# A hybrid decoder step on one core: output projection by halves of the tokens, per-layer projection in two parts, and a last FFN group of four tiles

## The chip, the core and the metric

The kernel runs on one core of one Trainium2 chip. Its engines are TensorE (PE in the profile, with its weight loads as PEld), VectorE (DVE), ScalarE (ACT), GpSimd (POOL) and SyncE (SP); all DMAs of this kernel are started on SP's queue. The metric is the device time of one execution in microseconds (us); less is better.

## The reference

One layer of a decoder step for 1024 prompt tokens and 8 sample tokens, 1032 columns in all, with a model width of 1024. Two branches (a Mamba-2 SSD and a gated delta net, GDN) are projected, gated and merged. Then follow an output projection with a residual, a SwiGLU FFN of width 2816, an embedding per layer and a final norm. The end of the layer, where the change lies:

```python
mix = (g_ssm * jnp.einsum('ble,ed->bld', y.astype(dtype), w_branch_ssm)
       + g_gdn * jnp.einsum('ble,ed->bld', o.astype(dtype), w_branch_gdn))
x = x + jnp.einsum('bld,de->ble', mix, w_out)

gu = jnp.einsum('bld,df->blf', _rms_norm(x, norm_ffn), w_ffn_in)
gt, up = jnp.split(gu, 2, axis=-1)
x = x + jnp.einsum('blf,fd->bld', jax.nn.silu(gt) * up, w_ffn_out)

pe = jnp.einsum('blp,pd->bld', p, w_pl_proj)
x = x + pe * jax.nn.sigmoid(jnp.einsum('bld,de->ble', _rms_norm(x, norm_pl), w_pl_gate))
```

## The kernel before

**Layout.** Activations lie with the channels on the 128 partitions and the 1032 tokens (`NT`) along the free axis; 1024 channels are 8 tiles. Every product is made in three matmuls: each operand is split in a high part (rounded to `float32r`) and a low remainder, and high x high, high x low and low x high are summed in PSUM. `dense` does this for one block of 128 output columns, by chunks of tokens: `CHUNKS` are three of 344, `PARTS` are 384, 384 and 264. A block's sums go to PSUM tiles `pd` (three banks); the other PSUM pools are `pt` (2), `py` (2) and `pz` (1).

**Weights.** `load_w` loads a block of weights into a tile `wraw` (two buffers) and `split_raw` makes a high part `wh` on ACT and a low part `wl` on DVE, four 128x128 blocks at a time, with three buffers of each. This is done at a raised priority.

**Order of the work.** The tile framework makes the order of each engine's instructions ahead of the run, from the order of the code, the priorities and its own model of the costs; on the chip each engine and each queue then runs its list in order, and waits on semaphores.

**The stages around the change**, in the order of the code:

1. `ssm_branch(3, yacts)`: the last quarter of the SSM branch product. `load_o` loads the eight GDN outputs `o` and their gates, multiplies and splits them.
2. Branch merge: for each of 8 output blocks, the gates `sg_d` are loaded, the block's product with `w_branch_gdn` is made, and the merged block is split into `macts` (tiles `mx`). `residual` loads and transposes the input `x` into `acc`, called `x2` from here on.
3. Output projection: for each `f` of 8, `dense(load_w(w_out...), macts, ev)`, the sum added to `x2`. `squares` sums the squares of the channels for the norm: ACT squares, POOL adds into `sqs` (the last block's go to `rb`). Between the blocks, `embed` loads the per-layer embeddings by 128 tokens (`pr`), transposes and splits them into `pacts`.
4. `roots`: POOL adds `sqs` to `rb`, PE sums over the partitions with a matrix of ones, ACT takes the root and DVE the reciprocal.
5. The per-layer projection: for each of 8 blocks a product of `pacts` with `w_pl_proj`, copied by ACT to the tile `pe` and stored to `pe_d` in DRAM, to be read in the last stage.
6. FFN input. The product of the normed `x2` with `w_ffn_in` is made by a Strassen-like scheme on 2x2 blocks (halves of the channels and halves of the tokens, `HALF`, 516 tokens each): seven products instead of eight for each of the `NF` = 22 column tiles. Its seven operands are `b11`, `b21`, `bt1` to `bt4` and `b22`. `put` splits an operand (ACT, then DVE); the sums and differences are made on POOL. This preparation is a loop over `k` of 4, with single-buffered tiles `n1`, `n2`, `t1` to `t4`. `ffn_in(i)` makes the weights' combinations and the seven products, in chunks of 258; `product` takes the PSUM banks in turn from the list `spaces`. `b11` and `b21` need the first half of the tokens alone, and the first two products (`w11`, `w12`) need only these.
7. FFN output: after `ffn_in(i)` for even `i` from 2, `ffn_out(i - 2)` multiplies a pair of tiles `gu` (three buffers in the pool `gp`) with `w_ffn_out` and adds to `x2`. The last group (tiles 20 and 21) is a loop of its own with `PARTS`; there `gain_split` makes the operands `h3` of the next stage and the squares of the last-but-one norm.
8. The gate product with `w_pl_gate` (weights `gw`), the sum of `pe` times its sigmoid, and the final norm.

`bq` are two large tiles in the place of the two tiles `o`; `b11`, `b21`, `bt2` and `bt3` are their quarters. `pacts` lies in the quarter `bt3`, and is overwritten there once the per-layer projection is done with it.

## Time and profile before

| | us |
|---|---|
| median of 3 runs | 2696.67 |
| lowest and highest of them | 2696.55, 2699.24 |
| the profiled execution | 2692.9 |
| its span, first to last instruction | 2691.2 |
| output projection, start and end | 1715 to 1808 |
| last FFN group, first to last matmul | 2540.5 to 2577.8 |

Mean granted TensorE clock over the span: 0.987. DMA: 306.50 MB, mean 114 GB/s.

How to read the rows in this document. In a page's busy times the share is of the span. In a table by window, each row has the window, its length, the busy time of each engine with its number of instructions, the granted TensorE clock, the mean busy share of the 16 DMA engines and GB/s. In a list of waits, `A <- B: us, times, longest us` says that A's engine sat idle until B. In a timeline or a chain, a row has a start, a length, the engine, the line of the kernel, the operation, output<-inputs, the shape and a count, and in brackets the idle time ahead and what ended it. Groups of instructions give count, then busy time in us, the mean of one in ns, and the idle time ahead. Matmuls overlap, so a price is taken from start to start or over a long row.

### The profile page before, as it was taken

How to read it: one execution, taken by the hardware profiler on the slowest of the kernel's cores; microseconds unless marked ns; L12 is line 12 of the kernel's file. 1: busy time of each engine (PE TensorE's matmuls, PEld its weight loads, DVE VectorE, ACT ScalarE, POOL GpSimd, SP SyncE). 2: the span in 40 equal slices, each digit the busy share in tenths (PEclk: the TensorE clock that was granted, in tenths of full speed). 3: DMA queues.
4: the chain of work that ended last, by engine and by line, in shares of the span. 5: the costliest groups of instructions: out<-in, count | busy, mean ns of one | idle time of the engine just before them, and what ended most of it. 6: DMA issues, size and time to landing. Idle time of an engine off the chain costs nothing.

```text
span 2691.2 us, 46064 instructions
## 1 busy us (share of the span) xinstructions
PE 2591.2 (96%) x17959; PEld 2500.6 (93%) x17959; DVE 1761.8 (65%) x3217; ACT 1104.2 (41%) x2304; POOL 400.1 (15%) x599
## 2 busy tenths in 40 slices
PE   7999999999999999999999999996999999999988
PEld 7999999989989899898999999996999999999988
DVE  6677897588557576565445565337766666666775
ACT  5555555455364373343342234324322222322343
POOL 0111222121110110210000000025111111111020
PEclk9999999999999999999999999997999999999999
DMA  3345445445453453477664366222211111111132
GB/s 124 118 153 171 132 163 150 106 116 161 103 133 114 106 148 104 104 203 205 189 192 141 116 193 195 81 70 81 59 48 48 48 58 54 48 48 48 42 90 94
DMA packets 457384, 306.50 MB, mean 114 GB/s; under 512 B 44753, under 2 KB 430714, under 8 KB 456142
## 3 DMA queue, kind: packets, MB, share of 16 engines
q1 hardware_dynamic: 454766, 295.13, 38.0%
q10 hardware_dynamic: 2400, 8.42, 0.8%
q8 instruction: 142, 2.33, 0.4%
q14 instruction: 76, 0.62, 0.1%
HBM read 227.17 MB, written 76.31 MB: 113 GB/s over the span
## 4 chain that ended last, share of the span: by engine, by line
PE 62%; DMA 6%; DVE 6%; ACT 4%; issue 1%; POOL 1%; SPq 1%; DVEq 0%; POOLq 0%; ACTq 0%
PE pd L69 44%; PE py L69 7%; PE pt L69 6%; PE pz L69 3%; DMA ab<-acum_d 2%; ACT ab L709 1%; DVE wl L139 1%; DMA out_dram<-so 1%; ACT wh L138 1%; DVE bq L1220 1%; ACT sdt L613 0%; DMA sg<-gate_d 0%; DMA srb<-rn_d 0%; DVE sd L614 0%; DMA at<-at_d 0%
## 5 line engine op out<-in xcount | busy, mean ns | idle before, releaser
L69 PE MATMUL pd<-h,wh 128*128 128x344 f32 x4272 | 1041.1, 325 | 15.6 <-ACT wh L138 9.1
L69 PEld LDWEIGHTS pd<-h,wh 128*128 128x128 f32 x4272 | 740.6, 189 | 28.3 <-ACT wh L138 11.4
L69 PE MATMUL pd<-h,wl 128*128 128x344 f32 x2136 | 691.9, 324 | 3.3 <-DVE wl L139 2.3
L139 DVE TENSOR_TENSOR wl<-wraw,wh 128x512 fp32r<-128x512 f32 (+1 forms) x346 | 244.2, 708 | 263.5 <-ACT wh L138 261.3
L138 ACT CAST wh<-wraw 128x512 fp32r<-128x512 f32 (+1 forms) x346 | 209.5, 608 | 502.8 <-PE pd L69 361.5
L69 PEld LDWEIGHTS pd<-h,wl 128*128 128x128 f32 x2136 | 404.2, 189 | 8.6 <-DVE wl L139 6.8
L69 PE MATMUL pd<-gu,wh 128*128 128x344 f32 (+2 forms) x1056 | 251.2, 321 | 11.3 <-DVE acc L1344 11.1
L69 PEld LDWEIGHTS pd<-gu,wh 128*128 128x128 f32 x1056 | 183.0, 189 | 13.1 <-DVE acc L1344 9.5
L69 PE MATMUL pd<-y,wh 128*128 128x344 f32 x768 | 185.3, 323 | 0.0
L69 PE MATMUL pd<-gu,wl 128*128 128x344 f32 (+1 forms) x528 | 169.8, 322 | 0.0
L1318 DVE TENSOR_TENSOR acc<-acc,pd 128x344 f32<-128x344 f32 x240 | 121.9, 511 | 59.3 <-PE pd L69 54.7
L69 PE MATMUL pd<-bq,wh 128*128 128x258 f32 (+1 forms) x624 | 130.1, 302 | 20.3 <-ACT pe L1214 12.0
L709 ACT ACTIVATE ab<-ab,ncolA 128x128 f32<-128x128 f32 x256 | 81.8, 391 | 137.9 <-POOL ab L705 137.8
L69 PEld LDWEIGHTS pd<-y,wh 128*128 128x128 f32 x768 | 132.4, 188 | 1.1 <-issue 0.2
L69 PEld LDWEIGHTS pd<-bq,wh 128*128 128x128 f32 x624 | 103.3, 197 | 24.4 <-ACT pe L1214 13.3
L422 ACT COPY raw<-pd 128x344 f32<-128x344 f32 x144 | 62.6, 438 | 151.4 <-PE pd L69 138.9
L69 PE MATMUL pd<-y,wl 128*128 128x344 f32 x384 | 123.8, 323 | 0.0
L69 PEld LDWEIGHTS pd<-gu,wl 128*128 128x128 f32 x528 | 99.7, 189 | 0.0
L69 PE MATMUL pd<-o,wh 128*128 128x344 f32 x384 | 93.8, 326 | 3.9 <-DVE o L186 1.8
L436 DVE SCALAR_TENSOR_TENSOR ca<-raw,cwm,ca 128x1056 f32<-128x1056 f32 x72 | 95.9, 1333 | 2.0
L436 DVE SCALAR_TENSOR_TENSOR ca<-raw,cwg,ca 128x1056 f32<-128x1056 f32 x72 | 96.7, 1343 | 0.8
L69 PE MATMUL pd<-h,gw 128*128 128x384 f32 (+1 forms) x576 | 95.4, 324 | 0.0
(480 smaller groups left out, 5187.4 us busy)
## 6 DMA issues: line engine op xcount, KB each, us to landing
wraw<-in_w_in_dram SPq DMA_DIRECT2D x88, 512.0 KB
ab<-acum_d SPq DMA_DIRECT2D x32, 512.0 KB
out_dram<-sd SPq DMA_DIRECT2D x48, 256.0 KB
ru<-in_w_ffn_in_dram SPq DMA_DIRECT2D x22, 512.0 KB
wraw<-in_w_ffn_in_dram SPq DMA_DIRECT2D x22, 512.0 KB
wro<-in_w_ffn_out_dram SPq DMA_DIRECT2D x80, 128.0 KB
sg_d<-mg SPq DMA_DIRECT2D x16, 516.0 KB
bb<-rk_d SPq DMA_DIRECT2D x8, 1024.0 KB
```

The lines of the kernel that those rows point to most:

```text
L69: TE.matmul(o, l, r, start=start, stop=stop)
L138: S.copy(wh[:, :n], raw[:, k0 : k0 + n])
L139: V.tensor_tensor(wl[:, :n], raw[:, k0 : k0 + n], wh[:, :n].bitcast(F32), ALU.subtract)
L422: S.copy(raw[:, 3 + t0 : 3 + t0 + n], o[:, :n])
L436: V.scalar_tensor_tensor(ca, raw[:, j : j + CONVN], w[j], ca, ALU.mult, ALU.add)
L709: S.activation(ab[:, h], ab[:, h], AF.Exp, bias=ncolA[:, c, h0 + h : h0 + h + 1])
L1220: V.tensor_tensor(q[:, 1, k], src, q[:, 0, k].bitcast(F32), ALU.subtract)
L1318: V.tensor_tensor(a, a, o, ALU.add)
```

## The change

- `squares`/`roots`: the addition of `sqs` and `rb` on POOL goes; PE adds them by two matmuls into one PSUM bank.
- The embeddings are loaded, transposed and split ahead of `ssm_branch(3)`, into two tiles `ple`, and stored in DRAM (`ple_d`); at the start of the output projection they are loaded back into the quarter `bt3`.
- The per-layer projection of blocks 0 to 3 stands between `ssm_branch(3)` and the branch merge (output in pairs of a tile `pe`), that of blocks 4 to 7 behind the output projection, with PSUM banks of three pools in turn (`fills`).
- The output projection runs twice over the 8 blocks, first for tokens 0 to 515 and then for the rest, each in two chunks of 258. Behind the first half, its roots are taken, the eight normed tiles of that half are made and put into `b11` and `b21`, and stored in DRAM (`n_d`).
- The preparation works on the second half alone: it loads the stored halves `n1`, `n2`, makes `m1`, `m2`, and from them the five other operands, in tiles with two buffers. Per `k`: three operations on DVE, three on POOL, five `put`.
- The first two products of FFN tiles 0 and 1 (`ffn_first`) stand directly behind this preparation in the code, ahead of the rest of `ffn_in(0)`.
- The last group takes four tiles (18 to 21) with four weight blocks each; `ffn_out(18)` goes. The tile `gu` of number 21 lies in the place of `rb` and `sqs` (tile `rs`), the gate weights and the last-but-one norm's tiles move.

The diff, cut to what matters (plain moves of `product` and `plus` out of `ffn_in` are left out):

```diff
-            ps = pd.tile([P, 512], F32, name="pd")
+            pool, name = (pd, "pd") if pools is None else pools[0]
+            if pools is not None:
+                pools.append(pools.pop(0))
+            ps = pool.tile([P, 512], F32, name=name)
...
+    pacts = []
+    for k in range(2):
+        t = part_tile("ple")
+        pacts.append((t[:, 0], t[:, 1], t))
+    for tt in range(9):
+        n = P if tt < 8 else NB
+        pr_ = b2.tile([P, 256], F32, name="pr", tag="xf")
+        dma(pr_[:n], p_prompt[0, 0, tt * P : tt * P + P, :] if tt < 8 else p_sample[0, :, 0, :])
+        t = pt.tile([P, 512], F32, name="pt")
+        ts = slice(tt * P, tt * P + n)
+        for k in range(2):
+            TE.transpose(t[:, k * P : k * P + n], pr_[:n, k * P : k * P + P], ident[:n, :n])
+            hilo(pacts[k][0][:, ts], pacts[k][1][:, ts], t[:, k * P : k * P + n])
+    for k in range(2):
+        dma(ple_d[k], pacts[k][2].bitcast(F32))
     ssm_branch(3, yacts)
...
+    def per_layer(f, pacts, t, pools):
+        def ev(t0, tn, o):
+            S.copy(t[:, t0 : t0 + tn], o)
+
+        dense(load_w(w_pl_proj[:, f * P : f * P + P], 2), pacts, ev, CHUNKS, pools)
+        dma(pe_d[f], t)
+
+    for f in range(4):
+        if f % 2 == 0:
+            pe_ = part_tile("pe", F32)
+        per_layer(f, [a[:2] for a in pacts], pe_[:, f % 2], None)
...
-        G.tensor_tensor(rb[:, ts], rb[:, ts], sqs[:, ts], ALU.add)
-        mm(t[:, :tn], ones, rb[:, ts])
+        mm(t[:, :tn], ones, sqs[:, ts], True, False)
+        mm(t[:, :tn], ones, rb[:, ts], False, True)
...
+    rs = nrm.tile([P, 2, NT], F32, name="rs")
+    rb, sqs = rs[:, 0], rs[:, 1]
...
     QT = NT // 2
+    QC = QT // 2
...
+    b11, b21, bt2, bt3 = bq[0][:, 0], bq[0][:, 1], bq[1][:, 0], bq[1][:, 1]
+    pv = bt3.rearrange("p h (k two) t -> p h k (two t)", two=2)
     pacts = [(pv[:, 0, k], pv[:, 1, k]) for k in range(2)]
...
-        dense(load_w(w_out[:, f * P : f * P + P], 8), macts, ev)
-        if f < 7:
-            squares(f, sqs, rb, 0, NT, b2)
-        if 1 <= f < 6:
-            embed(2 * f - 2)
-            if f < 5:
-                embed(2 * f - 1)
+    for k in range(2):
+        dma(pv[:, :, k].bitcast(F32), ple_d[k])
+
+    def put(q, k, src):
+        S.copy(q[:, 0, k], src)
+        V.tensor_tensor(q[:, 1, k], src, q[:, 0, k].bitcast(F32), ALU.subtract)
+
+    def scaled(dst, j, ts):
+        V.scalar_tensor_tensor(dst, x2[:, j, ts], gain(G_FFN, j), rb[:, ts], ALU.mult, ALU.mult)
+
+    for hf in range(2):
+        parts = tuple((hf * QT + c * QC, QC) for c in range(2))
+        for f in range(8):
+            def ev(t0, tn, o):
+                a = x2[:, f, t0 : t0 + tn]
+                V.tensor_tensor(a, a, o, ALU.add)
+                if f == 7:
+                    squares(f, sqs, rb, t0, tn, b2)
+
+            dense(load_w(w_out[:, f * P : f * P + P], 8), macts, ev, parts)
+            if f < 7:
+                squares(f, sqs, rb, hf * QT, QT, b2)
+        for t0, tn in parts:
+            roots(sqs, rb, t0, tn)
+        if hf == 0:
+            for k in range(4):
+                for q, j in ((b11, k), (b21, k + 4)):
+                    n = b2.tile([P, QT], F32, name="n", tag="sg")
+                    scaled(n, j, HALF[0])
+                    put(q, k, n)
+                    dma(n_d[j], n)
...
+    firsts = {}
+
+    def ffn_first(i, rg):
+
+        x1 = sqs[:, HALF[0]] if i == 1 else ft.tile([P, QT], F32, name="x1")
+        g1 = ft.tile([P, QT], F32, name="g1", bufs=2)
+        with tc.high_priority(offset=2000):
+            w11 = split_raw(rg[:, 0:4], 4)
+        product(w11, b11, lambda ts, o: S.copy(x1[:, ts], o))
+        with tc.high_priority(offset=2000):
+            w12 = split_raw(rg[:, 4:8], 4)
+        product(w12, b21, plus(g1, x1))
+        firsts[i] = x1, g1
...
+    with tc.tile_pool(name="prep", bufs=2, side="right", reuse_waits="tile") as prep:
+        fills = [(pd, "pd"), (py, "py"), (pd, "pd"), (py, "py"), (pd, "pd"), (pz, "pz")]
+        for f in range(4, 8):
+            per_layer(f, pacts, prep.tile([P, NT], F32, name="pe", bufs=1), fills)
         for k in range(4):
-            n1 = prep.tile([P, NT], F32, name="n1")
-            n2 = prep.tile([P, NT], F32, name="n2")
-            for j, n in ((k, n1), (k + 4, n2)):
-                V.scalar_tensor_tensor(n, x2[:, j], gain(G_FFN, j), rb, ALU.mult, ALU.mult)
-            put(b11, k, n1[:, HALF[0]])
-            put(b21, k, n2[:, HALF[0]])
-            t1 = prep.tile([P, QT], F32, name="t1")
-            G.tensor_tensor(t1, n1[:, HALF[1]], n1[:, HALF[0]], ALU.subtract)
-            t2 = prep.tile([P, QT], F32, name="t2")
-            G.tensor_tensor(t2, n2[:, HALF[1]], t1, ALU.subtract)
+            m1, m2, n1, n2, t2 = (prep.tile([P, QT], F32, name=n) for n in ("m1", "m2", "n1", "n2", "t2"))
+            dma(n1, n_d[k])
+            dma(n2, n_d[k + 4])
+            scaled(m1, k, HALF[1])
+            V.tensor_tensor(n1, m1, n1, ALU.subtract)
+            scaled(m2, k + 4, HALF[1])
+            G.tensor_tensor(t2, m2, n1, ALU.subtract)
+            G.tensor_tensor(n2, n2, t2, ALU.subtract)
+            G.tensor_tensor(m1, m2, m1, ALU.subtract)
+            put(bt1, k, n1)
+            put(b22, k, m2)
             put(bt2, k, t2)
-            t3 = prep.tile([P, QT], F32, name="t3")
-            G.tensor_tensor(t3, n2[:, HALF[1]], n1[:, HALF[1]], ALU.subtract)
-            put(bt3, k, t3)
-            t4 = prep.tile([P, QT], F32, name="t4")
-            G.tensor_tensor(t4, n2[:, HALF[0]], t2, ALU.subtract)
-            put(bt4, k, t4)
-            put(bt1, k, t1)
-            put(b22, k, n2[:, HALF[1]])
+            put(bt4, k, n2)
+            put(bt3, k, m1)
+        with tc.high_priority(offset=2000):
+            early = [gate_rows(0), gate_rows(1)]
+        for i in range(2):
+            ffn_first(i, early[i])
...
-            w11 = split_raw(a11, 4)
-            w12 = split_raw(a12, 4)
+        if i not in firsts:
+            ffn_first(i, rg)
...
+        g_ = nrm.tile([P, 2, NT], F32R, name="gu", tag="rs") if i == NF - 1 else gp.tile([P, 2, NT], F32R, name="gu")
...
-        if i >= 2 and i % 2 == 0:
+        if i >= 2 and i % 2 == 0 and i < NF - 2:
             ffn_out(i - 2)
...
-        wt = load_w(w_ffn_out[(NF - 2) * P :, f * P : f * P + P], 2)
-        dense(wt, [gacts[NF - 2], gacts[NF - 1]], ev, PARTS)
+        wt = load_w(w_ffn_out[(NF - 4) * P :, f * P : f * P + P], 4)
+        dense(wt, [gacts[i] for i in range(NF - 4, NF)], ev, PARTS)
...
-                pool, tag = (slb, "parts") if f < 5 else (gp, "gu")
+                pool, tag = (slb, "parts") if f < 4 else (gp, "gu") if f < 7 else (nrm, "rs")
```

More of the change, by code (lines that the diff above doesn't have):

```diff
@@ L257, in hybrid_step @@
     vb_d = dr.tile([8, P, NC, P], F32, name="vb_d")
+    ple_d = dr.tile([2, P, 2, NT], F32, name="ple_d")
+    n_d = dr.tile([8, P, NT // 2], F32, name="n_d")
     bcd_d = dr.tile([2, 4, NB, P], F32, name="bcd_d")
@@ new lines, in hybrid_step, with product @@
+    spaces = [(pd, "pd"), (py, "py"), (pd, "pd"), (py, "py"), (pd, "pd"), (pz, "pz"), (pt, "pt"), (pt, "pt")]
+    def product(w, b, *evs):
+        for c in range(2):
+            pool, name = spaces.pop(0)
+            spaces.append((pool, name))
+            o = pool.tile([P, 512], F32, name=name)[:, :QC]
+            for k in range(4):
+                h, l = (b[:, j, k, QCH[c]] for j in range(2))
+                mm(o, w[k][0], h, k == 0, False)
+                mm(o, w[k][0], l, False, False)
+                mm(o, w[k][1], h, False, k == 3)
+            for ev in evs:
+                ev(QCH[c], o)
@@ new lines, in plus, with gate_rows @@
+    def plus(dst, a):
+        return lambda ts, o: V.tensor_tensor(dst[:, ts], a[:, ts], o, ALU.add)
+    def gate_rows(i):
+        rg = wp.tile([P, 8, P], F32, name="wraw")
+        dma(rg, w_ffn_in[:, i * P : i * P + P].rearrange("(k p) f -> p k f", p=P))
+        return rg
+    firsts = {}
[9 more added lines that the diff above has]
+        firsts[i] = x1, g1
```

73 lines of the change are left out of this document (11 added, 62 removed).

## The prediction

> **What bounds the kernel now.** I read the page's busy times first, then the busy times by window, to find where TensorE (PE) isn't full.
>
> ```profile
> PE 2591.2 (96%) x17959; PEld 2500.6 (93%) x17959; DVE 1761.8 (65%) x3217; ACT 1104.2 (41%) x2304; POOL 400.1 (15%) x599
> ...
> PEclk9999999999999999999999999997999999999999
> ```
>
> PE carries the kernel. What can be won is time in which PE is idle or at a lower granted clock, and every matmul added is paid in full. Three of the windows below leave PE unfilled (the first row is there for its DMA share, the third is full).
>
> ```profile
> core 0: us, PE busy (x) PEld busy (x) DVE busy (x) ACT busy (x) POOL busy (x), PEclk, DMA share, GB/s
> 1580.00:1590.00 10.00, 10.00 (x65) 10.00 (x65) 4.32 (x8) 4.71 (x6) 0.00 (x0) 1.00 0.96 310
> 1606.00:1625.00 19.00, 15.07 (x86) 12.85 (x85) 14.62 (x17) 9.15 (x11) 1.45 (x3) 0.98 0.85 288
> 1715.00:1808.26 93.26, 93.26 (x593) 91.79 (x592) 27.57 (x59) 21.45 (x44) 16.36 (x8) 1.00 0.15 44
> 1808.26:1882.00 73.74, 51.29 (x251) 45.46 (x250) 57.22 (x52) 34.71 (x72) 36.68 (x23) 0.81 0.29 99
> 2540.50:2577.80 37.30, 26.04 (x147) 24.21 (x145) 35.07 (x42) 21.78 (x27) 13.42 (x5) 0.94 0.32 96
> ```
>
> 1606 is the start of the GDN branch product, 1715 to 1808.26 the output projection, 1808.26 to 1882 the passage into the FFN, 2540.5 to 2577.8 the last FFN group. PE's waits from 1590 on name who holds it; the first lies in the passage, the second in the last group:
>
> ```profile
> PE pd L69 <- ACT pe L1214: 12.0, 5, 4.7
> PE pd L69 <- DVE acc L1344: 11.1, 5, 5.3
> ```
>
> Prices of PE work, from the chain (344 and 258 columns) and PE's timeline (root sums):
>
> ```profile
> 1739.62 9.76 PE pd L69 x62
> 1883.25 1.44 PE py L69 x12
> ...
> 2582.58 0.81 PE L69 MATMUL pt<-rb,ones 128*128 128x384 f32 x2
> 2582.93 5.00 PE L69 MATMUL pd<-h,gw 128*128 128x384 f32 x26
> 2592.61 0.61 PE L69 MATMUL pt<-rb,ones 128*128 128x264 f32 x2
> 2592.86 7.36 PE L69 MATMUL pd<-h,gw 128*128 128x384 f32 x40
> ```
>
> 344 columns cost 9.76/62 = 0.157 us and 258 cost 1.44/12 = 0.120; along that line 384 cost 0.174 and 264 cost 0.123. A root sum holds PE from its start to the next one's: 0.35 us at 384, 0.25 at 264.
>
> **The change, part 1: the passage (T0 = 1808.26).** Useful PE work in the 73.7 us: 8 per-layer products of 18 matmuls (144 x 0.157 = 22.6), 96 FFN matmuls (11.5), three root sums (1.0); so 38.6 us are lost. VectorE (DVE) and GpSimd (POOL) pace it:
>
> ```profile
> 1816.81 2.30 DVE L1157 RECIPROCAL rb<-rb 128x344 f32<-128x344 f32 x1
> 1828.98 0.68 DVE L1220 TENSOR_TENSOR bq<-n,bq 128x516 fp32r<-128x516 f32 x1
> 1829.58 1.76 DVE L1220 TENSOR_TENSOR bq<-t,bq 128x516 fp32r<-128x516 f32 x1
> 1831.26 0.68 DVE L1220 TENSOR_TENSOR bt<-t,bt 128x516 fp32r<-128x516 f32 x1
> 1881.94 0.68 DVE L1220 TENSOR_TENSOR b<-n,b 128x516 fp32r<-128x516 f32 x1
> ...
> 1822.86 1.27 POOL L1232 TENSOR_TENSOR t<-n,t 128x516 f32<-128x516 f32 x1
> 1829.20 1.59 POOL L1230 TENSOR_TENSOR t<-n 128x516 f32<-128x516 f32 x1 [1.90 <-DVE n L1226]
> ...
> L1226 DVE SCALAR_TENSOR_TENSOR n<-acc,gcols,rb 128x1032 f32<-128x1032 f32 x8 | 10.1, 1285 | 1.4 <-POOL t L1235 1.4
> ```
>
> A subtraction of 516 columns takes a slot of 0.60 us (1828.98 to 1829.58), and 1.68 (to 1831.26) when a POOL operation runs beside it: each POOL operation costs DVE about 1.1 us. Counting so from the end of the last reciprocal (1819.1) to the last put (1882.6): 8 scalings x 1.22, 28 puts x 0.61, 9 weight splits (4.8), 22 POOL operations x 1.1: 56 us. It took 63.5, 1.13 times that; the rest is waiting.
>
> The Trainium skill says more ("SBUF — State Buffer", section "Who interferes with whom"): a DVE instruction with two SBUF inputs and a POOL instruction that reads SBUF exclude each other for the whole instruction. By that rule each pair would cost DVE the full 1.27 us of a POOL operation, and the sum at the end would be 3 us smaller. The slots of 1.68 rather than 0.60 + 1.27 = 1.87 agree with the block but let a little overlap, so I keep 1.1.
>
> After the change the first half's eight scalings and sixteen puts stand beside the second half of the output projection: 46 us of PE, against DVE's splits (16 x 0.61), sums (16 x 0.35), reciprocals (2 x 1.73), 16 preparation operations (9.8) and six POOL sums, some 35 us; covered. Behind T0 remain, for the second half: 8 scalings of 516 and 4 subtractions, 20 puts (32 x 0.61 = 19.5), 12 POOL operations, plus 7 splits and 4 sums (5.4) and 5 POOL operations for the first FFN weights: 24.9 + 17 x 1.1 = 43.6, times 1.13 = 49.3 us. It starts when the last reciprocal ends; with chunks of 258 (1.73 us each) and no POOL addition ahead of the root sum I take T0 + 5, against T0 + 10.8 now. It ends at T0 + 54.3.
>
> PE has meanwhile four per-layer products (11.3), two FFN tiles' first two products (96 x 0.120 = 11.5), and, as three weight buffers allow three open products, three quarters of three more (54 x 0.120 = 6.5), and 0.5 of roots: 29.8. Loss 24.5; gain **14.1**. The wait on the per-layer output stays: its tile still has one buffer and a copy waits for the store (below), about 3.8 + 1.1 us per product against 2.8 of PE; six PSUM banks hide it until T0 + 11, and later PE waits for DVE anyway. The loads of the stored halves queue on SP behind those stores; two buffers and 8 us a step cover them, else they lengthen the 49 us.
>
> ```profile
> 1813.96 3.69 DMA pe_d<-pe
> ...
> 1817.73 1.14 ACT L1214 COPY pe<-pd 128x344 f32<-128x344 f32 x3 [1.29 <-DMA pe_d<-pe]
> ```
>
> **Part 2: additions to PE.** The output projection runs 8 x 96 matmuls of 258 for 8 x 72 of 344: 92.2 against 90.4, **-1.8**. Root sums become two matmuls each: eight of about 0.25 and 2 x (0.35 + 0.35 + 0.25), 3.9 against 2.0: **-1.9**. Its weights are loaded and split twice (8 more DMAs of 512 KB where the DMA share is 0.15). The second weight buffer comes free half a chunk ahead of a set's end and is needed half a chunk into the next: 2.9 us where it was 3.8, and a cast, a split and their waits take 1.3 alone and 2.4 beside POOL. No row shows a miss; bounds 0 and -5 (16 sets, a few behind a 1.7 us slot), I take **-2**, as the FFN runs with the same 2.9 us and PE full.
>
> **Part 3: entry of the GDN branch.**
>
> ```profile
> 1606.78 0.48 PE L69 MATMUL pd<-o,wh 128*128 128x344 f32 x2
> 1623.35 0.42 PE L69 MATMUL pd<-o,wh 128*128 128x344 f32 x1 [0.53 <-DVE o L187]
> 1625.01 0.94 PE L69 MATMUL pd<-o,wh 128*128 128x344 f32 x2 [0.19 <-DVE sg L1129]
> ```
>
> The first column block takes 18.2 us for 72 matmuls (11.3) and 0.9 of transposes: 6 lost, waiting for operands whose loads fill the DMA engines (share 0.96, 310 GB/s). The change puts 1.8 us of transposes and 11.3 of per-layer products ahead of it as cover, but also loads 1.0 MB of embeddings, stores 2.1 MB of their split, loads 0.5 MB of weights and stores 2.1 MB of products: at 310 GB/s 11.8 us, or 18.6 with the last stores. The last operand then comes at 1635 to 1642, and the block ends 1.7 later, where PE alone would need until 1632. So the loss is 5 to 12 instead of 6; if the stores fall behind the loads it is 0. Bounds +6 and -6; I take **-1**. The per-layer products themselves only move.
>
> **Part 4: the last group.** Useful PE work in its 37.3 us: 8 x (12 x 0.174 + 6 x 0.123) = 22.6; 14.7 lost. By groups and, for a sum alone, the output projection's:
>
> ```profile
> L1338 DVE SCALAR_TENSOR_TENSOR h<-acc,gcols,h 128x1032 fp32r<-128x1032 f32 x7 | 12.3, 1760 | 0.0
> L1344 DVE TENSOR_TENSOR acc<-acc,pd 128x384 f32<-128x384 f32 x16 | 8.4, 546 | 0.6 <-PE pd L69 0.5
> ...
> 1798.95 2.42 POOL L1148 TENSOR_TENSOR sqs<-sqs,sqt 128x1032 f32<-128x1032 f32 x1 [9.63 <-ACT sqt L1147]
> ```
>
> DVE is busy 35 of 37 us: the bound. Afterwards PE has 45.2 us here (22.6 moved from where PE was full), while DVE needs 8 x (0.61 split + 1.3 adds + 1.2) = 24.9, six POOL sums (at most 2.4 each, 14.5) and some gate splits (3.5): 43. PE becomes the bound, narrowly; three PSUM banks hold 5.6 us, so I leave 3.4 of loss: **+11.3** (bounds 4 and 14). The 24 additions saved lay beside a full PE: nothing.
>
> **Sum.** 14.1 - 1.8 - 1.9 - 2 - 1 + 11.3 = 18.7 us. The profiled execution took 2692.9 (span 2691.2), so 2674.2; the median of the runs is 3.8 above it, 2696.67, and the same step gives **2678**.
>
> **The rivals.**
> - *The preparation is hidden* (0.15): POOL's waits for its operands spread its operations so that DVE pays little. Then 24.9 us end at T0 + 30, as PE's work does; the passage gains 36.5 instead of 14.1: 2656. For it: POOL idles half of the passage; against: the 1.68 slots.
> - *The preparation takes as long as now* (0.12): the reloads and stores on SP or the in-order puts replace the saved work by waits, 63 us as today. The passage gains 0, the sum is 4.6: 2692.
> - *The last group stays DVE-bound* (0.07): 2678 + 9 = 2687.
> - *Slower* (0.08), by the SP queue at the branch. Nine embedding loads go through two buffers, each waiting for transposes and splits, and the operand loads may queue behind them. Now two load together in each column block without haste, so no row prices the round. At 4.5 us a load one after another the operands come 40 us later, at 1663; the block ends 33 us behind PE, a loss of 33 instead of 6, and the sum falls to -7: 2704. It decides from 38 us of delay on (a loss of 31 eats the other 19.7 and the 0.2%). Against it: the buffers overlap, and 40 us of free PE work run ahead.
>
> **How the numbers follow.** The forecast holds 0.58, with 2664 to 2690 as its own range from the bounds (passage 8 to 25). For 8 in 10 the range goes to 2658 and 2692: most of the third case, half of the first. A change of 0.2% (5.4 us) is about what a measurement of this kernel can tell: faster 0.58 + 0.15 + 0.07 + 0.04 of the second rival = 0.84, the same 0.08, slower 0.08.
>
> **What would show it.** Right: PE full through the per-layer products behind the output projection, then idle on puts until about 54 us after its end (74 now); the output projection some 2 us longer plus roots; the last group's waits on the additions mostly gone and about 49 us long; POOL beside slots of 1.7 on DVE. Wrong: waits on weight splits in the second half's projection, the first GDN block ending later than 1.7 us behind a PE that never waited, or reloads of the stored halves among DVE's waits.

## The result, and the profile after

The changed kernel takes 2680.65 us (median; 2676.16 to 2687.23) where the kernel before takes 2696.67 beside it (2689.78 to 2700.72): the ratio is 0.9947, 95% interval 0.993 to 0.9964, so 10 to 19 us are gained. The profiled execution took 2679.36 us (span 2677.7). The forecast was 2678. Two executions in the experiments below had a low granted clock and are in no ratio, one of the last group alone (2742.67 us, clock 0.899) and one of the preparation on DVE (8255.67 us, clock 0.35, the profiled one).

The page of the changed kernel, busy times and granted clock:

```profile
PE 2584.4 (97%) x18167; PEld 2498.6 (93%) x18167; DVE 1760.6 (66%) x3226; ACT 1113.7 (42%) x2317; POOL 389.4 (15%) x595
...
PEclk9999999999999999999999999999999999999999
```

The slice of clock 0.7 in the passage is gone (over the whole passage the clock goes from 0.81 to 0.84, by the rows below and those of the prediction). To see where the time went, I cut both executions at the same matmuls: those that read `y` (end of the SSM branch), `o` (GDN branch), `mx` (output projection) and `gu` (FFN output). Rows of the tiles' matmuls, first of the kernel before, then of the changed one; the two times at the end are the starts of the first and the last:

```profile
L69 PE MATMUL pd<-y,wl x384: 315/320/426, 1358.0 to 1606.6; 128*128 128x344 f32 x192
L69 PE MATMUL pd<-o,wl x192: 317/320/488, 1607.1 to 1712.1; 128*128 128x344 f32 x192
L69 PE MATMUL pd<-mx,wl x192: 313/319/427, 1713.7 to 1808.1; 128*128 128x344 f32 x192
L69 PE MATMUL pd<-gu,wh x1056: 280/319/689, 1930.6 to 2577.4; 128*128 128x344 f32 x160, 128*128 128x384 f32 x15, 128*128 128x264 f32 x1
L69 PE MATMUL pd<-gu,wl x528: 283/321/522, 1930.9 to 2577.6; 128*128 128x344 f32 x160, 128*128 128x384 f32 x15, 128*128 128x264 f32 x1
```

```profile
L69 PE MATMUL pd<-y,wl x384: 315/320/427, 1358.9 to 1611.6; 128*128 128x344 f32 x192
L69 PE MATMUL pd<-o,wl x192: 316/320/488, 1623.4 to 1735.7; 128*128 128x344 f32 x192
L69 PE MATMUL pd<-mx,wl x256: 278/282/390, 1737.2 to 1833.1; 128*128 128x258 f32 x128
L69 PE MATMUL pd<-gu,wh x1056: 280/319/342, 1930.9 to 2563.2; 128*128 128x344 f32 x144, 128*128 128x384 f32 x24, 128*128 128x264 f32 x8
L69 PE MATMUL pd<-gu,wl x528: 282/321/339, 1931.2 to 2563.4; 128*128 128x344 f32 x144, 128*128 128x384 f32 x24, 128*128 128x264 f32 x8
```

Cut at these times, with 11.3 us of per-layer products (72 matmuls) that moved from the passage into the GDN branch's stretch:

| stretch | before | after | difference | without the moved 11.3 |
|---|---|---|---|---|
| start to the last `y` | 1606.6 | 1611.6 | +5.0 | +5.0 |
| to the last `o` (GDN branch) | 105.5 | 124.1 | +18.6 | +7.3 |
| to the last `mx` (output projection) | 96.0 | 97.4 | +1.4 | +1.4 |
| to the first `gu` (passage) | 122.5 | 97.8 | -24.7 | -13.4 |
| to the last `gu` (FFN) | 647.0 | 632.5 | -14.5 | -14.5 |
| to the end | 113.6 | 114.3 | +0.7 | +0.7 |
| span | 2691.2 | 2677.7 | -13.5 | -13.5 |

At the first `gu` the two kernels are level (1930.6 and 1930.9): up to there the change gave with one hand and took with the other, and the last group decides. The first row is not all the change's: in the profiled executions of this document, the same instructions up to the last `y` ended anywhere from 1606.6 to 1615.6 without the embeddings ahead of it (six executions, mean 1611.1), and from 1608.3 to 1617.2 with them (seven, mean 1613.9). The means differ by 2.8; 1.8 of it are the 18 transposes.

The same stretches in the busy times by window, changed kernel (first row: end of `y` into the GDN branch; then the first GDN block, the output projection, the passage, the last group):

```profile
core 0: us, PE busy (x) PEld busy (x) DVE busy (x) ACT busy (x) POOL busy (x), PEclk, DMA share, GB/s
1600.00:1650.00 50.00, 39.11 (x234) 37.13 (x233) 28.30 (x40) 25.02 (x40) 1.24 (x4) 0.92 0.84 294
1623.10:1647.20 24.10, 13.45 (x82) 12.02 (x80) 11.78 (x13) 11.16 (x13) 0.19 (x1) 0.90 0.88 310
1735.00:1833.20 98.20, 97.41 (x801) 96.50 (x800) 52.20 (x86) 37.59 (x66) 15.56 (x12) 1.00 0.43 132
1833.20:1885.70 52.50, 36.01 (x212) 34.39 (x210) 48.01 (x46) 23.94 (x50) 33.38 (x20) 0.84 0.42 132
2518.20:2563.50 45.30, 45.30 (x290) 45.30 (x290) 30.70 (x42) 23.14 (x26) 12.91 (x5) 1.00 0.37 114
```

Now the output projection and the last group have PE full; the first GDN block has it busy for 13.45 of 24.10 us. PE's waits from 1550 to 2680 say who held it:

```profile
PE pd L69 <- DVE sg L1162: 8.4, 1, 8.4
PE pd L69 <- ACT bq L1208: 6.5, 1, 6.5
PE pz L69 <- ACT pe L1118: 4.8, 1, 4.8
PE py L69 <- ACT pe L1118: 3.9, 1, 3.9
...
PE pt L1103 <- DMA pr<-in_p_prompt_dram: 1.0, 1, 1.0
...
PE pd L69 <- DVE wl L139: 0.8, 1, 0.8
```

The longest one is new. It is the first GDN block, whose three open chunks wait for the merge gate `sg`. DVE's, SP's and PE's timelines of the changed kernel show the chain:

```profile
1636.37 1.23 DVE L190 TENSOR_TENSOR o<-lt,o 128x1032 fp32r<-128x1032 f32 x1 [0.52 <-ACT o L189]
...
1646.66 1.35 DVE L1162 TENSOR_TENSOR sg<-sg,pd 128x344 f32<-128x344 f32 x3
...
1628.16 0.32 SPq L1084 DMA_DIRECT2D lt<-og_d  x1
...
1635.88 0.38 SPq L146 DMA_DIRECT2D wraw<-in_w_branch_gdn_dram  x1
...
1636.98 0.38 SPq L1154 DMA_DIRECT2D lt<-sg_d  x1
1637.40 1.22 SPq L1158 DMA_DIRECT2D sg<-sg_d  x1
...
1647.22 0.94 PE L69 MATMUL pd<-o,wh 128*128 128x344 f32 x2 [8.36 <-DVE sg L1162]
```

The last operand is split at 1636.37 + 1.23 = 1637.6, but the gates' loads are only issued at 1637.0 and 1637.4, behind the last operand load (1628.16) and a weight load (1635.88) on the one in-order queue. The gate is there 9 us later.

### The profile page after: what moved, and what is told of

It is laid out like the page before. It is cut to its first block, busy times and chain, and to the rows that moved or that the text cites. A ratio compares the mean times of both kernels' runs of the same rounds, so it can differ in the third digit from the quotient of the medians.

```text
span 2677.7 us, 46537 instructions
## 1 busy us (share of the span) xinstructions
PE 2584.4 (97%) x18167; PEld 2498.6 (93%) x18167; DVE 1760.6 (66%) x3226; ACT 1113.7 (42%) x2317; POOL 389.4 (15%) x595
## 4 chain that ended last, share of the span: by engine, by line
PE 63%; DMA 7%; DVE 3%; ACT 3%; POOL 2%; issue 2%; SPq 1%; DVEq 0%; POOLq 0%; ACTq 0%
PE pd L69 46%; PE py L69 7%; PE pt L69 6%; PE pz L69 3%; DMA ab<-acum_d 3%; DMA out_dram<-so 1%; ACT ab L714 1%; ACT wh L138 0%; DMA mg<-y_d 0%; DVE wl L139 0%; ACT sdt L618 0%; DMA at<-at_d 0%; DMA DB<-dd_d 0%; POOL ab L710 0%; POOL Xt L766 0%
## 5 line engine op out<-in xcount | busy, mean ns | idle before, releaser
L139 DVE TENSOR_TENSOR wl<-wraw,wh 128x512 fp32r<-128x512 f32 (+1 forms) x362 | 255.0, 706 | 273.0 <-ACT wh L138 268.2
L138 ACT CAST wh<-wraw 128x512 fp32r<-128x512 f32 (+1 forms) x362 | 221.4, 614 | 486.9 <-PE pd L69 329.1
L69 PE MATMUL pd<-gu,wl 128*128 128x344 f32 (+2 forms) x528 | 169.2, 320 | 0.0
L1360 DVE TENSOR_TENSOR acc<-acc,pd 128x344 f32<-128x344 f32 x216 | 109.7, 511 | 53.5 <-PE pd L69 49.2
L69 PE MATMUL pd<-bq,wh 128*128 128x258 f32 (+1 forms) x560 | 107.4, 288 | 7.8 <-ACT bq L1208 6.5
L69 PEld LDWEIGHTS pd<-bq,wh 128*128 128x128 f32 x560 | 88.4, 192 | 8.8 <-ACT bq L1208 7.0
```

The source lines that it names most:

```text
L69: TE.matmul(o, l, r, start=start, stop=stop)
L138: S.copy(wh[:, :n], raw[:, k0 : k0 + n])
L139: V.tensor_tensor(wl[:, :n], raw[:, k0 : k0 + n], wh[:, :n].bitcast(F32), ALU.subtract)
L1360: V.tensor_tensor(a, a, o, ALU.add)
```

## The experiments

All ratios are to the kernel before, with the 95% interval; each stretch is cut as above. A difference of 3 us between two kernels is inside the intervals of their times, so the stretches carry the argument. Each is read from one execution. Where an edit doesn't touch a stretch, it repeats within 0.2 us in the passage (97.8 four times, 94.7 and 94.9 with the embeddings back), 0.6 in the FFN with four tiles in its last group (632.4 to 633.0) and 2.4 in the branch (115.1 and 112.7 with the stores late). Only the way to the last `y` scatters by 9.

| kernel | ratio | last `y` | GDN branch | output projection | passage | FFN | rest |
|---|---|---|---|---|---|---|---|
| before | 1 | 1606.6 | 105.5 | 96.0 | 122.5 | 647.0 | 113.6 |
| changed | 0.9947 (0.993 to 0.9964) | 1611.6 | 124.1 | 97.4 | 97.8 | 632.5 | 114.3 |
| last group alone | 0.9966 (0.9953 to 0.9978) | 1614.1 | 106.7 | 96.0 | 122.6 | 633.0 | 115.2 |
| gates early | 0.9945 (0.9931 to 0.9959) | 1608.3 | 123.2 | 97.6 | 97.8 | 632.7 | 114.3 |
| operands first | 0.995 (0.9938 to 0.9963) | 1615.0 | 122.2 | 97.6 | 97.8 | 632.4 | 114.3 |
| stores late | 0.9906 (0.9893 to 0.992) | 1612.5 | 115.1 | 97.2 | 97.8 | 632.5 | 114.3 |
| embeddings back | 0.9948 (0.9933 to 0.9964) | 1609.8 | 104.9 | 121.3 | 94.7 | 632.5 | 115.2 |
| same, output in `xf` | 0.991 (0.9895 to 0.9924) | 1615.6 | 105.1 | 112.5 | 94.9 | 632.5 | 115.5 |
| preparation on DVE | 0.9932 (0.9918 to 0.9945) | 1615.6 | 123.0 | 98.2 | 92.8 | 632.4 | 114.3 |
| two `pe` tiles | 0.9952 (0.9939 to 0.9965) | 1616.9 | 123.3 | 97.9 | 97.7 | 632.5 | 114.3 |
| back, on DVE | 0.9907 (0.9894 to 0.9921) | 1613.6 | 104.6 | 112.4 | 93.2 | 632.5 | 115.3 |
| back, on DVE, two tiles | 0.9888 (0.9875 to 0.9902) | 1606.7 | 104.3 | 113.2 | 90.8 | 632.5 | 114.5 |
| stores late, on DVE, two tiles | 0.9886 (0.9866 to 0.9906) | 1617.2 | 112.7 | 98.3 | 91.6 | 632.5 | 114.3 |

In the kernels with the embeddings back, the 11.3 us of per-layer products stand in the output projection, in the others made from the changed kernel in the GDN branch.

**The last group alone.** The kernel before with this one edit (and the tiles that it needs):

```diff
-        if i >= 2 and i % 2 == 0:
+        if i >= 2 and i % 2 == 0 and i < NF - 2:
             ffn_out(i - 2)
...
-        wt = load_w(w_ffn_out[(NF - 2) * P :, f * P : f * P + P], 2)
-        dense(wt, [gacts[NF - 2], gacts[NF - 1]], ev, PARTS)
+        wt = load_w(w_ffn_out[(NF - 4) * P :, f * P : f * P + P], 4)
+        dense(wt, [gacts[i] for i in range(NF - 4, NF)], ev, PARTS)
```

> The kernel before with only the last part of the change: the last output group has four tiles instead of two. Theory A: the last group alone is worth 13.5 to 14 us, its loss falling from 14.7 to about 0.5: 0.9949 of the kernel before, 2683, and everything ahead of 2490 is unchanged; then the rest of the change (passage +13, branch entry -8, output projection and roots -4) nets to about zero. Theory B: it is worth the 11.3 us that were forecast (0.9958, 2685.4) and the other three came from the passage. Theory C: its gain depends on what lies ahead of it, and alone it brings under 8 us.

The FFN stretch takes 633.0 us for 647.0, as in the changed kernel (632.5), and the group has PE full for all but 0.28 us:

```profile
2526.70:2572.50 45.80, 45.52 (x289) 45.21 (x289) 29.97 (x42) 22.95 (x26) 12.88 (x5) 1.00 0.36 108
```

So theory A's 14 us stand in their stretch, and there theory C falls. The comparison of times gives 9 us (6 to 13): that is less than the stretch, excludes A's 0.9949 and by itself would not exclude C. Of the gap between the two, 1.6 us are lost again in the rest and 1.2 in a branch that this edit doesn't touch; where the remainder went is not shown. The other parts of the change are then worth 0.9966 to 0.9947 of the time, some 5 us by the ratios; by the stretches 325.3 - 319.3 = 6.0 us from the last `y` to the first `gu`, of which the way to the last `y` takes back 2.8. Not nothing, then, but little.

**Embeddings back.** The changed kernel without the embeddings ahead of the GDN branch: they are made after blocks 1 to 5 of the output projection's first half, and per-layer products 0 to 3 ride in its second half:

```diff
-    for k in range(2):
-        dma(ple_d[k], pacts[k][2].bitcast(F32))
...
+            if hf == 0 and 1 <= f < 6:
+                embed(2 * f - 2)
...
+            if hf == 1 and f in (1, 3, 5, 6):
+                per_layer((1, 3, 5, 6).index(f), pacts, b2.tile([P, NT], F32, name="pe", tag="sg"), None)
```

> The changed kernel, but the nine embedding tiles are made as before: between the column blocks of the output projection (of its first half), straight into bt3, with no store and reload of them, and the four per-layer products ride in the second half of the output projection instead of ahead of the GDN branch. Theory A: the entry of the GDN branch lost about 7 us more than the -1 that was forecast, because SP's in-order queue issues the merge gates' loads 20 us later than before (1637 for 1617), behind the operand loads and a weight load that wait for DVE. Then without the embeddings the first GDN block takes 18 us again instead of 24, y ends 5 us earlier, PE stays full in the output projection, which has DVE busy for 52 of 98 us, and the time is 6 to 8 us below the changed kernel: about 2673, 0.9915 of the kernel before. Theory B: the block is late for another reason (operand bytes that must come anyway), or the embeddings cost as much again between the output blocks: within 2 us of the changed kernel, 0.994 to 0.9955.

The time is theory B's, the mechanism theory A's: the branch takes 104.9 us (124.1 - 11.3 = 112.8 in the changed kernel), 8 us won, and the output projection loses them again. Of its 121.3 us, some 110 are accounted for (96.5 from the first to the last of its matmuls in the changed kernel, 11.3 of per-layer products, 1.8 of transposes); the rest is mostly one wait, between 1715 and 1836:

```profile
PE pd L69 <- ACT pe L1102: 8.8, 1, 8.8
```

ACT's timeline shows the copy that it waited for, right behind the last split of the first half, whose eight tiles `n` turn in the same two buffers (`sg`) and are stored from them:

```profile
1790.22 0.62 ACT L1196 CAST bq<-n 128x516 fp32r<-128x516 f32 x1 [1.80 <-DVE n L1200]
1790.75 1.13 ACT L1102 COPY pe<-pd 128x344 f32<-128x344 f32 x3
```

The products were there at 1782 and held all three banks of `pd` until a tile came free. That was my choice of buffer. Here the output goes to another one, and the products come behind the fourth to seventh block:

```diff
-            if hf == 1 and f in (1, 3, 5, 6):
-                per_layer((1, 3, 5, 6).index(f), pacts, b2.tile([P, NT], F32, name="pe", tag="sg"), None)
+            if hf == 1 and f in (3, 4, 5, 6):
+                per_layer(f - 3, pacts, b2.tile([P, 9, P], F32, name="pe", tag="xf").rearrange("p a b -> p (a b)")[:, :NT], None)
```

> The first experiment (embeddings back between the column blocks of the output projection, no store and reload of them) with one thing mended: the four per-layer products of the second half write into the buffers of xf, which nothing else uses by then, instead of those of sg, where their copies stood behind the eight stores of n and held all three PSUM banks; and they come after the fourth to seventh block instead of the second. Theory A: that wait of 8.8 us was all that the first experiment lost in the output projection, and the entry of the GDN branch had given back its 8 us; so the output projection with four per-layer products and 18 transposes takes 96.5 + 11.3 + 1.8 = 110 us instead of 120, and the time is 8 to 10 us below the changed kernel: 0.991 to 0.992 of the kernel before, about 2671. Theory B: the wait only moves (the stores of per-layer rows or the weights on SP's queue), and the time stays within 3 us of the changed kernel.

0.991, theory A: 2674 us, branch 105.1, output projection 112.5. What the entry of the GDN branch lost is the price of what the change put ahead of it: the embeddings, four per-layer products and the stores of both.

**Why the entry loses: order or bytes.** First the order of the loads. The gates of the first GDN block in a tile of their own, far ahead:

```diff
+    with tc.high_priority(offset=2000):
+        g0 = part_tile("g0", F32)
+        for j in range(2):
+            dma(g0[:, j], sg_d[8 * j])
...
-        sg = b2.tile([P, NT], F32, name="sg")
-        dma(sg, sg_d[8 + f])
+        sg = g0[:, 1] if f == 0 else b2.tile([P, NT], F32, name="sg")
+        if f > 0:
+            dma(sg, sg_d[8 + f])
```

> The changed kernel with the merge gates of the first GDN block (lt and sg of f = 0) in a tile of their own, loaded ahead of the operand loads that wait, instead of in the two shared buffers of lt and sg. Nothing else is moved: the embeddings and the per-layer products stay ahead of the GDN branch. Theory A: PE's wait of 8.4 us on sg is a wait for these two loads; it goes, and what is left is the last operand, which 1.0 MB more ahead of it may bring 3 us later: first block ends at 1639 to 1643 instead of 1647, time 4 to 8 us below the changed kernel, 0.992 to 0.993 of the kernel before. Theory B: the operands are what is late (the DMA engines are at 0.88 of their time), and the wait moves to o: within 1.5 us of the changed kernel.

The wait on `sg` is gone, and the branch takes 123.2 us all the same. PE's waits from 1600 to 1650 are now on the operands, 8.1 us where the gate had cost 8.4:

```profile
PE pd L69 <- ACT o L189: 3.6, 1, 3.6
PE pd L69 <- DVE o L190: 3.3, 1, 3.3
PE pd L69 <- DVE o L189: 1.2, 1, 1.2
```

Theory B. Then the weights behind the operands as well:

```diff
-        with tc.high_priority(offset=2000):
+        with tc.high_priority(offset=ahead):
...
-        dense(load_w(w_branch_gdn[:, f * P : f * P + P], 8), oacts, ev)
+        dense(load_w(w_branch_gdn[:, f * P : f * P + P], 8, 2000 if f > 1 else 60), oacts, ev)
```

> The changed kernel with the gates of the first GDN block in a tile of their own (as in the experiment before), and the weight loads of the first two GDN blocks no longer issued far ahead: on SP's queue they now stand behind the operand and gate loads. Theory A: the last operand is late because SP, in order, stands at weight loads whose buffer waits for a split on VectorE (16.1 us of such waits between 1600 and 1650 with the gates early, 12.8 in the changed kernel, 7.3 before the change); with the operands first the last one comes 5 to 8 us earlier, the first block ends at 1634 to 1638 instead of 1647, and the time is 7 to 10 us below the changed kernel, 0.991 to 0.992. Theory B: the DMA engines carry what they can (13 MB in 45 us, 0.84 to 0.88 of their time), the order of the issues changes nothing, and weights that come later are one more wait: the changed kernel's time or up to 3 us more.

Branch 122.2 us; now the weights are late, and the last operand is no earlier: its split starts at 1639.5, 24.5 us after the last `y`, in the changed kernel at 1636.4, 24.8 us after it. DVE's and PE's timelines:

```profile
1639.54 1.22 DVE L190 TENSOR_TENSOR o<-lt,o 128x1032 fp32r<-128x1032 f32 x1
```

```profile
1638.06 1.51 PE L69 MATMUL pd<-o,wh 128*128 128x344 f32 x4 [10.50 <-ACT wh L138]
```

Whichever load is put ahead, another becomes the last: gate, operand, weight, each time for 8 to 10.5 us. That speaks for bytes. SP's waits at weight loads, the cause that theory A named, had hardly grown with the change: between 1600 and 1650 they are 11.7 us in the kernel before and 12.8 in the changed one (the expectation's 7.3 is of the window 1590 to 1640). So the six stores were moved behind the first two GDN blocks in the code:

```diff
-    for k in range(2):
-        dma(ple_d[k], pacts[k][2].bitcast(F32))
...
-        dma(pe_d[f], t)
+        if f < 4:
+            late.append((pe_d[f], t))
+        else:
+            dma(pe_d[f], t)
...
+        if f == 1:
+            for d, s in late:
+                dma(d, s)
```

> The changed kernel with its six stores at the entry of the GDN branch (two of the split embeddings, 2.1 MB, and four of per-layer products, 2.1 MB) issued from the second GDN block on, instead of among the operand loads. All else stays, the order of the loads too. Theory A: the entry is bound by the bytes that the DMA engines move before the last operand and gate are there (0.84 of their time, 294 GB/s between 1600 and 1650); 4.2 MB less ahead of them are 13.5 us at 310 GB/s, the first block's loss falls from 12.8 us to at most the 6 of the kernel before, and the time is 7 to 10 us below the changed kernel: 0.991 to 0.992 of the kernel before, as the forecast said for stores behind the loads. Theory B: it is the chain of buffers, splits and issues on one queue that is long (two buffers for lt and sg, embeddings between the operands on VectorE), and bytes are not short; then it stays within 2 us of the changed kernel.

0.9906, 11 us below the changed kernel by the ratios, 9 of it in the branch: 115.1 - 11.3 = 103.8 us, less than before the change. The busy times of this kernel by window:

```profile
1600.00:1650.00 50.00, 46.27 (x283) 45.47 (x282) 32.33 (x46) 25.00 (x41) 2.39 (x5) 0.97 0.88 290
```

The DMA engines move as much in these 50 us as in the changed kernel (290 and 294 GB/s), but what PE needs comes first: PE is busy for 46.3 us instead of 39.1, and its one listed wait in the first block is 3.7 us, on an operand. On the chip, though, the stores moved less far than in the code, and the order of the loads did not stay as it was. SP's timeline:

```profile
1611.15 0.43 SPq L1169 DMA_DIRECT2D ple_d<-ple  x1
...
1630.73 0.32 SPq L1160 DMA_DIRECT2D sg<-sg_d  x1
...
1639.70 0.38 SPq L146 DMA_DIRECT2D wraw<-in_w_branch_gdn_dram  x1
...
1640.76 2.70 SPq L1169 DMA_DIRECT2D pe_d<-pe  x4
```

One store of the embeddings (1 MB) still stands ahead of the last operand load (1623.2), the other behind the gate `sg`; only the four of per-layer products (2.1 MB) come behind both gates. The gates, in turn, now stand ahead of a weight load that they stood behind in the changed kernel. Counted from the last `y`, the last operand's split starts 22.9 us after it instead of 24.8, and the first product with the gate 27.1 instead of 35.1, so most of what is won lies in the gate. Shown: with the stores later in the code the entry loses nothing against the kernel before. Not told apart: whether it was their bytes or the places in SP's queue. SP's waits at weight loads are no part of it, at 12.8 us as in the changed kernel.

**The passage.** The preparation's GpSimd work on VectorE:

```diff
-            G.tensor_tensor(t2, m2, n1, ALU.subtract)
-            G.tensor_tensor(n2, n2, t2, ALU.subtract)
-            G.tensor_tensor(m1, m2, m1, ALU.subtract)
+            V.tensor_tensor(t2, m2, n1, ALU.subtract)
+            V.tensor_tensor(n2, n2, t2, ALU.subtract)
+            V.tensor_tensor(m1, m2, m1, ALU.subtract)
```

> The changed kernel with the twelve GpSimd subtractions of the preparation (three per k) on VectorE. Theory A (forecast's slot model): a GpSimd operation costs VectorE 1.1 us of blocked time, and done by VectorE itself it costs 0.61; the preparation ends 12 x 0.5 x 1.13 = 6.7 us earlier (last put 46 us after the output projection's end instead of 52.5), and the time falls by 5 to 7 us: 0.9925 of the kernel before. Theory B: GpSimd works mostly beside VectorE, which loses little by it; then the preparation takes 12 x 0.61 = 7.3 us more on VectorE, and the time rises by about 7 us: 0.997.

The ratio was 0.994 (0.9926 to 0.9954): neither theory's time, and no profile that could say why. Once more:

> The kernel with the preparation's twelve GpSimd subtractions on VectorE once more, for a profile in which the clock is not disturbed. Its time before was 2680.5, the changed kernel's own, so neither theory's time came (5 to 7 us less, 7 more). Theory A now: the preparation does end some 6 us earlier, and PE waits for something else (the per-layer output's tile, the reload of the stored halves), so that T0 to the first FFN output stays at 98 us. Theory B: GpSimd's price to VectorE is about 0.61 us an operation instead of 1.1, and the last put comes where it came, 52.5 us after the end of the output projection.

The last put ends at 1882.66 + 0.68 = 1883.3, 46.4 us after the end of the output projection (1836.9), where the slot model said 46. DVE's timeline, the last put:

```profile
1882.66 0.68 DVE L1209 TENSOR_TENSOR bq<-m,bq 128x516 fp32r<-128x516 f32 x1
```

The passage takes 92.8 us for 97.8: 5.0 of the 6.1 us reach PE. For the preparation and the passage that is the slot model (theory A of the first of the two expectations); that the passage would stay at 98 us, as the second one had it, was wrong. The times gain less than the 5 to 7 us of theory A: 0.994 and 0.9932 for 0.9947 are 2 and 4 us, though the interval of the second (0.9918 to 0.9945) reaches that far. The Trainium skill ("SBUF — State Buffer", section "SBUF: two separate sides") has such a pair exclude each other for a whole instruction. At 1.27 us an operation this step would have brought 12 x (1.27 - 0.61) x 1.13 = 8.9 us, by an estimate from this case's rows. The 6.1 us measured lie nearer to the 6.7 that 1.1 gives.

Two tiles for the per-layer output:

```diff
-            per_layer(f, pacts, prep.tile([P, NT], F32, name="pe", bufs=1), fills)
+            per_layer(f, pacts, sqs if f % 2 else prep.tile([P, NT], F32, name="pe", bufs=1), fills)
```

> The changed kernel with two tiles in turn for the output of the per-layer products behind the output projection (the second one is the buffer of the sums of squares, free by then). Theory A (forecast): PE's waits on that copy, 9.6 us between 1847 and 1870, cost nothing, since PE waits afterwards for the preparation in any case, and the wait of 6.5 us on bq at 1880 grows by what they shrink; the preparation's last put stays at 52.5 us after the output projection's end: within 2 us of the changed kernel. Theory B: products that come earlier let the FFN's first tiles come earlier too and the preparation has slack: up to 9 us faster, 0.9915.

The waits on `pe` are gone, and the passage takes 97.7 us for 97.8: PE waits for the preparation instead, and for weights whose split stands behind it on DVE. The two longest waits from 1833 to 1935:

```profile
PE pd L69 <- ACT bq L1208: 8.0, 1, 8.0
PE pt L69 <- DVE wl L139: 5.1, 1, 5.1
```

**Together.**

> The kernel with the embeddings back between the output blocks (0.991) and, besides, the preparation's twelve GpSimd subtractions on VectorE. Alone the one gave about 9 us, the other 3 to 5 (the passage 92.8 us instead of 97.7). If they add up: 2668 to 2671, 0.9885 to 0.990 of the kernel before. If they don't, since with less traffic PE waits for the per-layer output's tile (15.4 us of waits on its copy in the passage): 0.991 again.

> The same with two tiles in turn for the output of the last four per-layer products. If with the preparation on VectorE its end (46 us after the output projection's) still sets the passage, the second tile brings nothing, as it brought nothing alone, and the time is that of the run beside it within 2 us. If the copies now are what is late, it brings 2 to 5 us more: 0.987 to 0.989.

> The kernel with the six stores late (0.9906), and in the passage the twelve GpSimd subtractions on VectorE and two tiles in turn for the per-layer output. If the two places are independent, the branch takes 115 us as with the late stores and the passage 91 to 93 instead of 97.8: 5 to 7 us below that kernel, 2664 to 2666, 0.988 to 0.989 of the kernel before. If the stores that now come later meet the reloads of the passage, the passage stays above 95 us and the time above 2668.

With the embeddings back, the preparation on VectorE brought only 1.7 us in the passage (94.9 to 93.2) and nothing in the ratio: PE waited for the `pe` copies (10.4 us there, none with the second tile). There the second tile, worth 0.1 us alone, brought 2.4 (90.8), and the ratio fell to 0.9888. The route with the late stores ends at the same place, 0.9886 (2666.84 us): branch 112.7, passage 91.6, as was expected of two places that don't depend on each other. Each is some 16 us faster than the changed kernel; which is the faster of the two stays open.

## Why the prediction was right, and where it wasn't

The forecast of 18.7 us met 16.0 by the medians, and 13.5 by the spans of the two profiled executions. The passage was priced right. That the sum fits as well is in part luck: the GDN branch came out 7 us worse than forecast, the last group 3 and the additions to PE some 2 better, and the way to the last `y` scatters by more than either.

- **Passage, +14.1 forecast, 13.4 measured.** The slot model held: the last put ended at 1885.7, 52.5 us after the end of the output projection (forecast 54.3), the last reciprocal 5.0 us after it (forecast 5), by DVE's timeline:

```profile
1834.78 3.39 DVE L1190 RECIPROCAL rs<-rs 128x258 f32<-128x258 f32 x2 [0.59 <-ACT rs L1189]
...
1885.02 0.69 DVE L1209 TENSOR_TENSOR bq<-m,bq 128x516 fp32r<-128x516 f32 x1
```

  The single `pe` tile cost nothing, as said, because PE waited for DVE in any case; the second tile alone showed it. So the sign "PE full through the per-layer products" did not come (PE waited 9.6 us there on the copies), though the sum held. The reloads of the stored halves are among none of PE's waits, nor of DVE's between 1833 and 1886.
- **Output projection, roots, weights: -1.8, -1.9, -2 forecast.** Its stretch grew by 1.4 us, though 1.8 of transposes had left it: 3.2, with the first half's roots in it. The weights cost 0.8 (one wait on `wl`), not 2. The loads and splits kept up.
- **GDN branch, -1 forecast, some -8 measured** (7.3 in the stretch, and about 1 of waits at the end of the `y` products). This step failed, and left its bounds of +6 and -6. The arrival was right by the clock: last operand at 1635 to 1642 forecast, 1637.6 measured, though 5.0 us of that are a later last `y`. "The block ends 1.7 later" was wrong, and with it a sign of being wrong came: the block ended at 1647.2, 9.6 us after its last operand. The step had priced the operands and not the gates, which the block needs too. These, which before were issued at 1617 to 1620, close behind the last operand load, now stood behind the stores and weights as well and came 9 us after the last operand. SP's timeline of the kernel before:

```profile
1615.22 0.32 SPq L1079 DMA_DIRECT2D lt<-og_d  x1
1617.33 0.32 SPq L1125 DMA_DIRECT2D sg<-sg_d  x1
...
1619.85 0.32 SPq L1121 DMA_DIRECT2D lt<-sg_d  x1
```

  "If the stores fall behind the loads it is 0" came near: with the stores late, most of them behind those loads, the branch is 1.7 us shorter than before.
- **Last group, +11.3 forecast, 14.5 measured.** PE became the bound as said, but without the loss of 3.4 us. The term that failed is DVE's need of 43 us: it took 30.7 of 45.3. Six POOL sums were charged to DVE in full, 14.5 us; the five in this stretch cost it 1.7. Why so little, the last section shows.
- **The rivals.** The preparation is not hidden: made 6 us shorter, it shortened the passage by 5. It doesn't take as long as before: 47.5 us from the last reciprocal to the last put, where it took 63.5. The last group isn't DVE-bound. The slower case put its mechanism in the right place, the entry of the GDN branch, but named the loads of the embeddings, where the experiments point at the stores, and needed 38 us of delay; the branch lost 7.

## What to carry to other kernels

Where transfers fill the DMA engines ahead of a stage, list every load that its first block needs (operands, gates, weights) and every byte issued before the last of them, stores too; here, stores moved later in the code paid 9 us, two other orders of the loads at most 2. A wait that costs nothing, like that on a tile with one buffer, can start to cost when the longer wait behind it is shortened, so it is worth trying again after each gain. A new tile that shares buffers with tiles that are stored takes over their delays.

## What the runs showed of the hardware

What a POOL operation costs DVE depends on where DVE's inputs lie. In the last group of the changed kernel, POOL's and DVE's timelines:

```profile
2532.35 2.57 POOL L1181 TENSOR_TENSOR sqs<-sqs,sqt 128x1032 f32<-128x1032 f32 x1 [33.50 <-ACT sqt L1180]
...
2551.27 2.50 POOL L1181 TENSOR_TENSOR sqs<-sqs,sqt 128x1032 f32<-128x1032 f32 x1 [5.01 <-ACT sqt L1180]
```

```profile
2532.55 0.55 DVE L1386 TENSOR_TENSOR acc<-acc,pd 128x384 f32<-128x384 f32 x1
...
2552.70 2.15 DVE L1450 TENSOR_TENSOR gw<-wraw,gw 128x1024 fp32r<-128x1024 f32 x1 [0.75 <-ACT gw L1449]
...
2555.12 1.21 DVE L1450 TENSOR_TENSOR gw<-wraw,gw 128x1024 fp32r<-128x1024 f32 x1
```

Beside the sum at 2532.35, an addition that reads one operand from PSUM (`pd`) took 0.55 us, as it does without POOL. Beside the sum at 2551.27, a split with both inputs in SBUF took 2.15 us instead of 1.21. Of the additions, scalings and splits of this stretch, only two were lengthened, both splits with two SBUF inputs that met a sum (2.15 and 2.01 us for 1.21). The Trainium skill says the same ("SBUF — State Buffer", section "Who interferes with whom"): a DVE instruction with at most one SBUF input does not contend with GpSimd, outside the faster modes.

The rule alone would not have given the number. In the kernel before, whose DVE was busy for 35 of 37 us, the same sums met splits and scalings. POOL's and DVE's timelines there:

```profile
2550.50 2.93 POOL L1148 TENSOR_TENSOR sqs<-sqs,sqt 128x1032 f32<-128x1032 f32 x1 [30.13 <-ACT sqt L1147]
```

```profile
2551.09 2.61 DVE L139 TENSOR_TENSOR wl<-wraw,wh 128x256 fp32r<-128x256 f32 x1
```

Such a split takes 0.42 us without POOL. Between 2551 and 2574 five sums lengthened five operations by 9.2 us in all, 1.8 us a sum, where the forecast charged 2.4 as the most. In the changed kernel DVE waits for PE, and beside three of the five sums it had only additions to do; the next operation with two SBUF inputs came after they were done. So what a sum costs depends on which operations it meets, and the forecast charged the meetings of the old order.
